# A hybrid attention and linear-attention layer in fp32 pairs on one core: both gate-weight splits in one unit, the last tile's splits and first eviction moved, and the first gates on VectorE

## The chip, the core and the metric

The kernel runs on one core of a Trainium2 chip. Its time is the device time of one execution in microseconds; the kernel before has three timed runs, and one further execution was profiled. In what follows TensorE (PE) multiplies matrices, ScalarE (ACT), VectorE (DVE) and GpSimd (POOL) do the elementwise work, and SyncE (SP) issues the DMAs.

## The reference, cut to what matters

One layer of a decoder takes 2048 prompt tokens (16 tiles of 128) and 8 sequences of 8 sampled tokens (64 rows, the seventeenth tile, called NB in the code).

```python
h = rms_norm(x, g_mix_pre)
proj = jnp.einsum('btd,de->bte', h, w_in)
q, k, v, gq, gk, gv, gr, glr = jnp.split(proj, points, axis=-1)
attn = swa_banded(q, k, v, sinks)                       # group A: window of 128, 8 heads, 2 kv heads
log_a = jax.nn.log_sigmoid(glr @ w_gk2 + b_gk) / 16
o, s_new = gla_chunked(gq, gk, gv, log_a, s0)           # group B: gated linear attention, 4 heads
o = rms_norm(o, g_gla) * jax.nn.silu(gr)                # the output gate
mix = concat([attn, o]) @ w_out
x = x + rms_norm(mix, g_mix_post)
x = x + rms_norm(mlp(rms_norm(x, g_ffn_pre)), g_ffn_post)
```

Everything is wanted in fp32. Each fp32 operand of a large product is kept as a high part, rounded to TensorE's format, and a low part, the remainder; a product is then three matmuls (high with high, high with low, low with high).

## The kernel before, in words

The kernel goes through four stages: attention on all tiles (group A), gated linear attention (GLA, group B) with the output projection at its end, the MLP's two halves, and their ends. TensorE, and in the attention stage ScalarE and VectorE too, go through their instructions in the order in which the program issues them (the class InOrder adds that order by hand). GpSimd, SyncE and, in the GLA stage, the plain ScalarE and VectorE instructions are ordered by a planner, which goes by the order of the program as a priority and by its own estimate of when an operand will be ready.

**Attention (L798 on).** Each tile has four units, two query heads each. A unit (`unit`, L466) is a generator of steps: copy the sinks into the score tile `s` (GpSimd), score products `sc`, row minima (VectorE), exponentials (ScalarE), normalisation (ScalarE and VectorE), transposes `pT`, the high part `ph` (ScalarE), the low part `pl` (VectorE), the value products `av` (which need `ph`, then `pl`), `rest` (ScalarE) and the output `mo`. The loop runs three units interleaved (`behind`, `now`, `ahead`), and between their steps it calls `run(fill, n)`: n matmuls of a list of products that need nothing of the units. In tiles 0 to 13 the list is the projections of later tiles; from tile 14 on it is `projecting` (L611), the products of GLA's columns. The letters T, A, X, S, B, C name places within a unit; the dictionary A_PLAN tells at which unit and letter each side task stands, so `klo0` (L449, the low part of the keys for the next tile: VectorE, then the copy on GpSimd, L451) at unit 3, T.

**Gate weights.** The weights of GLA's columns are in four chunks of 384 columns and eight rows of 128 (chunks 0 and 1 are G_EARLY, 2 and 3 G_LATE). From tile 3 on, each tile loads two raw pieces (`load_gw`, L255, two buffers `wg_raw`), and `split_some` (L767) splits one at unit 1, letter A, and one at unit 1, letter B. A split (L258) is a multiplication by the gain on GpSimd (L262), the copy to the high part on ScalarE, and the subtraction for the low part on GpSimd (L264), the last reader of the raw piece; for two pieces of chunk 0 and for all late ones it is one ScalarE and one VectorE instruction (L222). In the last tile (i = 15) one late piece is split at letter B of every unit, and each split issues the load of a further piece.

**`projecting`** makes one chunk of one tile's columns in 24 products and then evicts the PSUM bank on ScalarE, scaled by the row norms. Tiles 0 and 1 get chunks 0 and 1 within the attention stage and chunks 2 and 3 from its end on. The 64 sampled rows are computed with high and low rows side by side, and the eviction first folds the two (L211: ScalarE, then VectorE).

**Sampled units (L899).** Four further units attend over the caches of the sampled sequences. In the first unit of each half of the sequences the cached keys are transposed on TensorE and copied by ScalarE to `kc`, and the score products `ssc` need that copy.

**GLA (`gla`, L1123).** For each tile: transposes of q and k, seven level sums (`level_sums`, L1056: per level two ScalarE exponentials and two VectorE additions, each waiting for the other engine), the output gate (`gate`, L998: five steps on ScalarE and VectorE and two multiplications of 128x512 on GpSimd, L1007 and L1009), score products per level, their placement into AH and AT (VectorE, L1072 and L1183; the list `put` holds the copy to AT), the new state S (L1189), and the outputs `o`. The normalised and gated output `og` is transposed (`ogT`) in the next tile. `gla` yields numbers of products to be run between its parts (G_FILL = 34, 14, 16, 8, 20 and, for tile 0's first, 66). At the end of the first GLA tile the sampled rows' GLA (`gla_sample`, L1215) joins in as a side task; its gate is the same function. The instructions under `tc.issue_after(put[0].ins)` are ordered behind that instruction on its engine.

Of the kernel before, what the change touches and what calls it, by code (L numbers as in the profile page):

```python
# [15 lines left out]
AF = mybir.ActivationFunctionType  # L16
ALU = mybir.AluOpType
# [4 lines left out]
P = 128  # L22
# [3 lines left out]
NB = T // P  # L26
# [15 lines left out]
NL = len(LEVELS)  # L42
# [22 lines left out]
G_FILL = (34, 14, 16, 8, 20)  # L65
G_FIRST_FILL = 66
# [75 lines left out]
def hybrid_step_kernel(ctx: ExitStack, tc: tile.TileContext, I, O):  # L142
    nc = tc.nc
# [11 lines left out]
    def rows(i):  # L155
        return min(P, NTOK - i * P)
# [7 lines left out]
    te, ac, dv = (InOrder(tc, engine) for engine in (nc.tensor, nc.scalar, nc.vector))  # L164
# [4 lines left out]
    def bank(shape, kind, name):  # L169

        return ps.tile(shape, F32, tag=kind, name=name, bufs=1 if kind in "de" else 2)
# [25 lines left out]
    rstd_all = cpool.tile([P, NTILE], F32, name="rstd_all")  # L197
# [13 lines left out]
    def folded(out, p_, scalar=nc.scalar, vector=nc.vector):  # L211

        scalar.activation(out, p_[NS:], AF.Copy)
        vector.tensor_tensor(out, out, p_[:NS], op=ALU.add)  # L214
        return out
# [394 lines left out]

    def projecting(i, xT, chunks, act=nc.scalar):  # L611

        n = rows(i)
        for c in chunks:
            p_ = bank([P, 512], "a", f"gproj_{i}_{c}")
            _, wh, wl = gw[c]
            products = ((xT[1], wh), (xT[1], wl)) if i == NB else ((xT[0], wh), (xT[0], wl), (xT[1], wh))
            for k in range(KT):
                for u, (x, w) in enumerate(products):
                    te.matmul(  # L620
                        p_[:, :G_N], x[:, k, :], w[:, k, :],
                        start=k + u == 0, stop=k == KT - 1 and u == len(products) - 1,
                    )
                    yield
            if i not in gps:
                gps[i] = gp_pool.tile([P, G_W], F32, tag="gp", name=f"gp_{i}", bufs=2)
            out = gps[i][:n, c * G_N : (c + 1) * G_N]
            src = folded(out, p_[:, :G_N]) if i == NB else p_[:, :G_N]
            act.activation(out, src, AF.Copy, scale=rstd_all[:n, i : i + 1])
            projected.add((i, c))  # L630

    def load_cache(name, c):
# [45 lines left out]
    def run(products, n=None):  # L678
        deque(products if n is None else islice(products, n), 0)
# [87 lines left out]
    def split_some(n):  # L767

        for _ in range(min(n, len(weights))):
            c, k, raw, stage = weights.popleft()  # L770
            split_gw(c, k, raw)
            if stage and late:
                weights.append((*load_gw(*late.popleft(), *stage), stage))
# [3 lines left out]
    fill = chain.from_iterable(project(i, c) for i in range(2, NTILE) for c in range(2))  # L777
# [20 lines left out]
    for i in range(NB):  # L798
        if i + 4 < NTILE:
            load_x(i + 4)  # L800
        if i == NB - 1:
            wa_pool.release()
            w_pools.append(open_gw(G_LATE))
            for n in range(4):
                stage = ("w_raw", 2) if n % 2 else ("x", 2)
                weights.append((*load_gw(*late.popleft(), *stage), stage))
        elif i >= 3:
            for _ in range(min(2, len(early))):
                weights.append((*load_gw(*early.popleft()), None))
        store()  # L810
        if i == 4:
            nc.sync.dma_start(gain_d.rearrange("a d -> (a d)"), I["g_mix_post"][0])
            wgk, msk, smsk, dmsk, onehot, ggla = load_consts()
        if i == NB - 4:
            nc.sync.dma_start(smask, I["c_smask"])
            cached.update({(name, 0): load_cache(name, 0) for name in "kv"})
        if i >= NB - 2:
            t = i - NB + 2
            gxTs[t] = load_T(t, x_place(t))
            fill = chain(fill, projecting(t, gxTs[t], G_EARLY, ac))  # L820
        new = i + 3 < NTILE
        todo["turn"] = lambda: run(rotate(i + 1))
        if i + 2 < NTILE:
            todo["first"] = lambda: take_first(i + 2)
            todo["rest"] = lambda: todo.update(vl=take_rest(i + 2))
        if new:
            todo["junk"] = lambda: todo.update(rstd=x_norm(i + 3))

        def do(u, phase):
            for name, at in A_PLAN:  # L830
                if name == "x0" and i == 0:
                    at = 0, "C"
                if at == (u, phase) and name in todo:
                    todo.pop(name)()

        for u in range(4):
            next(now)
            do(u, "T")
            next(behind, None)
            next(now)  # L840
            do(u, "A")
            if u == 1 and i < NB - 1:
                split_some(1)
            later = next(queue)
            next(later)
            run(fill, A_FILL[u][0])
            next(behind, None)
            if u != 3:
                next(behind, None)
            run(fill, A_FILL[u][1])  # L850
            if u == 0:
                next(now)
            if u < 2 and new:
                hi, todo[f"x{u}"] = x_half(i + 3, u)
                hi()
            elif u == 2:
                todo.update(heads_T(i + 1))
            do(u, "X")
            run(fill, A_FILL[u][2])
            if u:  # L860
                next(now)
            do(u, "S")
            if u == 3:
                next(behind, None)
            next(behind, None)
            next(ahead)
            next(now)
            do(u, "B")
            if u == 1 or i == NB - 1:
                split_some(1)  # L870
            next(now)
            do(u, "C")
            behind, now, ahead = now, ahead, later
    for left in todo.values():
        left()
    store()
    fill = chain(fill, *(projecting(t, gxTs[t], G_LATE, ac) for t in G_FIRST))

    def ranks_T(pair, out):
# [18 lines left out]

    for n in range(4):  # L899
        later = next(queue, None)  # L900
        next(now)
        next(behind)
        if n == 0:
            cached["k", 1] = load_cache("k", 1)
        run(fill, 10)
        if n == 2:
            first_ranks()
        next(now)
        next(behind)
        next(behind)  # L910
        if n == 2:
            cached["v", 1] = load_cache("v", 1)
            z0 = first_decays()
        if later:
            next(later)
        run(fill, 13)
        next(now)
        next(behind, None)
        split_some(4)
        if ahead:  # L920
            next(ahead)
        next(now)
        behind, now, ahead = now, ahead, later
# [74 lines left out]
    def gate(i, gp, n):  # L998

        gr = gp[:n, 1024:1536]  # L1000
        t = next(sgs) if n == P else s_sg
        nc.scalar.activation(t[:n], gr, AF.Abs)
        nc.scalar.activation(t[:n], t[:n], AF.Exp, scale=-1.0)
        nc.scalar.activation(t[:n], t[:n], AF.Ln, bias=1.0)
        nc.vector.scalar_tensor_tensor(t[:n], gr, 0.0, t[:n], op0=ALU.min, op1=ALU.subtract)
        nc.scalar.activation(t[:n], t[:n], AF.Exp)
        nc.gpsimd.tensor_tensor(t[:n], t[:n], gr, op=ALU.mult)  # L1007
        t4 = t[:n].rearrange("p (h d) -> p h d", h=4)
        nc.gpsimd.tensor_tensor(t4, t4, ggla[:n].unsqueeze(1).to_broadcast([n, 4, P]), op=ALU.mult)  # L1009
        return t  # L1010

    def qk_T(i, gp, n, kind="d"):
# [110 lines left out]
    def gla(i, gp, og=iter(())):  # L1123
# [6 lines left out]
        kt = qk_T(i, gp, P)  # L1130
        dec = next(decs)
        following = decayed(i + 1) if i < NB - 1 else iter(())
        yield G_FILL[0] if i else G_FIRST_FILL, True
        deque(og, 0)
        put_diagonal(i, AH, gp, P)
        for l, b in enumerate(LEVELS):
            if l < NL - 1 or i == 0:
                level_sums(before, after, dec, l, b)
            else:
                with tc.issue_after(put[0].ins):  # L1140
                    level_sums(before, after, dec, l, b)
            if l == NL - 1:
                kd = next(kds)
                pair = i // 2 + 1 if i % 2 == 0 and i < NB - 2 else 0
                turned = keys_decayed(after, kt, next(kdTs), P, "e", kd, pair)
                nc.scalar.activation(dec[:, NL], before, AF.Exp, scale=1.0 / 16)
            weighted(XK, XQ, dec, kt, qz, l, b)
        next(turned)
        deque(following, 0)
        yield G_FILL[1], True  # L1150
        assert {(i, c) for c in range(4)} <= projected
        sg = gate(i, gp, P)
        yield G_FILL[2], True
# [284 lines left out]
    fill = chain(ending_, products())  # L1438
# [819 lines left out]
```

## Time and profile before

| what | us |
|---|---|
| median of three runs | 2193.89 |
| lowest and highest | 2193.14, 2196.88 |
| the profiled execution | 2193.01 |
| its span, first to last instruction | 2191.2 |
| TensorE busy in the span | 2156.9 |
| VectorE, ScalarE, GpSimd busy | 1530.7, 1219.1, 257.7 |

In the profile, L12 is line 12 of the kernel; an instruction is named by its output and inputs (`sc<-kh,qh`), and L131 is the line of the helper that issues everything that is ordered by hand. A row of a timeline gives the start, the duration, the engine, the line, the operation, the tiles and shapes, and in brackets the idle time of the engine before it with what ended it. A row of the view of waits gives who waited for what: total, times, longest. PE busy is counted from a matmul's start to the end of its result, and matmuls overlap; a short wait can hide under the one before.

### The profile page before, as it was taken

What the parts mean: (1) busy time and instruction counts of PE and PEld (TensorE: products, weight loads), DVE (VectorE), ACT (ScalarE), POOL (GpSimd) and SP (SyncE); (2) the same over time, 40 slices, a digit from 0 to 9 for tenths busy, and PEclk for the clock granted to TensorE, in tenths of its full rate; (3) what the DMA queues carried; (4) which work ended last, traced back from release to release, by engine and by line L of the source; (5) the groups of instructions that cost most, each with busy time, mean ns of one, the idle gap of its engine ahead of it and who ended that gap; (6) DMA issues with size and microseconds to landing.
All of it is one profiled execution on the core that took longest, in us unless ns stands there. A gap on an engine that the chain in (4) does not pass through costs nothing.

```text
span 2191.2 us, 34210 instructions
## 1 busy us (share of the span) xinstructions
PE 2156.9 (98%) x11784; PEld 1864.8 (85%) x11784; DVE 1530.7 (70%) x3199; ACT 1219.1 (56%) x2626; POOL 257.7 (12%) x414
## 2 busy tenths in 40 slices
PE   8999999999999999999999999999999999999998
PEld 7999989999998888788888887888888888888886
DVE  5988968777785765888888555548676666555566
ACT  5888867566664444555555544435445455444454
POOL 2566512121111100000000000000000000000000
PEclk9999999999999999999999999999999999999999
DMA  7344332224337765877777776758554433766685
GB/s 229 133 144 150 103 104 66 68 71 150 131 126 239 235 205 193 263 240 257 272 258 249 249 237 220 242 181 269 179 182 158 153 136 134 241 202 195 194 271 185
DMA packets 240314, 411.54 MB, mean 188 GB/s; under 512 B 25924, under 2 KB 142124, under 8 KB 236028
## 3 DMA queue, kind: packets, MB, share of 16 engines
q1 hardware_dynamic: 240140, 409.35, 56.6%
q8 instruction: 93, 1.52, 0.3%
q14 instruction: 81, 0.66, 0.1%
HBM read 265.82 MB, written 143.99 MB: 187 GB/s over the span
## 4 chain that ended last, share of the span: by engine, by line
PE 89%; ACT 3%; DVE 3%; DMA 2%; POOL 1%; issue 1%; SPq 0%; DVEq 0%; POOLq 0%; ACTq 0%
PE dn L131 27%; PE gproj L131 11%; PE uc L131 8%; PE uX L131 7%; PE out L1328 7%; PE proj L131 5%; PE ud L131 4%; PE ub L131 4%; PE ue L131 4%; PE sam L131 1%; PE dsam L131 1%; PE o L131 1%; PE sc L131 1%; PE out L131 1%; PE av L131 1%; PE pT L131 1%
## 5 line engine op out<-in xcount | busy, mean ns | idle before, releaser
L131 PE MATMUL dn<-o0t,o0s 128*128 128x512 f32 x896 | 349.3, 390 | 2.1 <-ACT f L2026 1.0
L131 PE MATMUL dn<-o1t,o0s 128*128 128x512 f32 x896 | 349.6, 390 | 0.7 <-DVE o1t L220 0.7
L131 PE MATMUL dn<-o0t,o1s 128*128 128x512 f32 x896 | 349.4, 390 | 0.0
L220 DVE TENSOR_TENSOR o1s<-rs,o0s 128x512 fp32r<-128x512 f32 x224 | 154.6, 691 | 230.9 <-ACT o0s L219 225.1
L219 ACT ACTIVATE o0s<-rs 128x512 fp32r<-128x512 f32 x224 | 141.1, 631 | 305.3 <-PE dn L131 285.4
L131 PE MATMUL gproj<-wg,gxh 128*128 128x384 f32 x1024 | 272.5, 342 | 0.3 <-DVE gp_s L214 0.3
L131 PEld LDWEIGHTS dn<-o0t,o0s 128*128 128x128 f32 x896 | 168.2, 188 | 39.8 <-ACT o0t L219 1.6
L131 ACT ACTIVATE st<-st 128x512 f32<-128x512 f32 x224 | 141.2, 630 | 106.7 <-DVE st L131 101.9
L131 PEld LDWEIGHTS dn<-o1t,o0s 128*128 128x128 f32 x896 | 168.2, 188 | 37.7 <-DVE o1t L220 1.9
L131 PEld LDWEIGHTS dn<-o0t,o1s 128*128 128x128 f32 x896 | 168.2, 188 | 35.3
L131 PE MATMUL uc<-H,s 128*128 128x512 f32 x768 | 187.8, 393 | 2.8 <-ACT st L131 2.8
L131 PEld LDWEIGHTS gproj<-wg,gxh 128*128 128x128 f32 x1024 | 183.8, 188 | 4.1 <-issue 3.1
L131 PE MATMUL gproj<-wg,gxl 128*128 128x384 f32 x576 | 186.0, 340 | 0.4 <-DVE gp_s L214 0.4
L131 PE MATMUL uX<-H,w 128*128 128x512 f32 x768 | 185.5, 390 | 0.0
L131 PEld LDWEIGHTS uc<-H,s 128*128 128x128 f32 x768 | 143.7, 189 | 33.6 <-ACT st L131 3.0
L131 PEld LDWEIGHTS uX<-H,w 128*128 128x128 f32 x768 | 144.4, 188 | 30.5
L220 DVE TENSOR_TENSOR o1t<-rt,o0t 128x512 fp32r<-128x512 f32 x224 | 153.1, 684 | 9.0 <-ACT o0t L219 9.0
L1328 PE MATMUL out<-wo,mt 128*128 128x512 f32 x680 | 158.6, 392 | 0.0
L209 POOL TENSOR_TENSOR frs<-rs_v,half 128x1 f32<-128x1 f32 (+1 forms) x13 | 10.1, 786 | 1208.7 <-DMA rt<-t_d 1119.0
L1328 PEld LDWEIGHTS out<-wo,mt 128*128 128x128 f32 x680 | 126.5, 188 | 26.1
L219 ACT ACTIVATE o0t<-rt 128x512 fp32r<-128x512 f32 x224 | 138.1, 618 | 12.0 <-DMA rt<-t_d 8.5
L131 DVE TENSOR_TENSOR st<-st 128x512 f32<-128x512 f32 x160 | 110.6, 691 | 28.5 <-ACT st L131 24.3
(405 smaller groups left out, 4306.9 us busy)
## 6 DMA issues: line engine op xcount, KB each, us to landing
s_d<-st SPq DMA_DIRECT2D x32, 1792.0 KB, 8.1
rs<-s_d SPq DMA_DIRECT2D x224, 256.0 KB, 2.9
raw<-in_w_up SPq DMA_DIRECT2D x64, 512.0 KB, 4.4
rt<-t_d SPq DMA_DIRECT2D x128, 256.0 KB, 3.9
rt<-in_w_down SPq DMA_DIRECT2D x96, 256.0 KB, 3.0
t<-in_w_down SPq DMA_DIRECT2D x64, 256.0 KB, 3.8
t_d<-t SPq DMA_DIRECT2D x32, 512.0 KB, 4.2
hraw<-h_d SPq DMA_DIRECT2D x20, 512.0 KB, 5.1
```

Source lines behind the costliest of these rows:

```text
L131: ins = call(*a, **k)
L209: nc.gpsimd.tensor_tensor(out, v[:n], e, op=ALU.pow)
L219: nc.scalar.activation(hi, src, AF.Copy)
L220: vector.tensor_tensor(lo, src, f32(hi), op=ALU.subtract)
L1328: te.matmul(banks[c], x, w[:, c * 512 : (c + 1) * 512], start=k + u == 0, stop=k == KT - 1 and u == len(products) - 1,)
```

## The change

Six edits. `projecting` holds back the eviction of tile 0's first chunk of each pair until three products of the following chunk are issued. In tiles 0 to 14 both splits stand at unit 1, letter A. In the last tile the four splits stand at letter B of the units 1, 2 (two) and 3. In the sampled units with an even number three of ten products go ahead of the score products. The two multiplications of `gate` go to VectorE for tile 0 and for the sampled rows. In `gla`, tile 1 runs three more products in its first part and three fewer in its second, and tile 2's level sums 4 and 5 join level 6 behind `put`.

```diff
     def projecting(i, xT, chunks, act=nc.scalar):
-        n = rows(i)
+        n, waiting = rows(i), []
         for c in chunks:
...
                     yield
+                    if waiting and (k, u) == (0, 2):
+                        act.activation(*waiting.pop(), scale=rstd_all[:n, i : i + 1])
...
-            act.activation(out, src, AF.Copy, scale=rstd_all[:n, i : i + 1])
+            if act is ac and (i, c) == (0, chunks[0]):
+                waiting.append((out, src, AF.Copy))
+            else:
+                act.activation(out, src, AF.Copy, scale=rstd_all[:n, i : i + 1])
             projected.add((i, c))
...
             do(u, "A")
             if u == 1 and i < NB - 1:
-                split_some(1)
+                split_some(2)
...
             do(u, "B")
-            if u == 1 or i == NB - 1:
-                split_some(1)
+            if u and i == NB - 1:
+                split_some(1 + (u == 2))
...
     for n in range(4):
         later = next(queue, None)
+        run(fill, 3 * (1 - n % 2))
         next(now)
         next(behind)
         if n == 0:
             cached["k", 1] = load_cache("k", 1)
-        run(fill, 10)
+        run(fill, 10 - 3 * (1 - n % 2))
...
-        nc.gpsimd.tensor_tensor(t[:n], t[:n], gr, op=ALU.mult)
+        engine = nc.vector if i in (0, NB) else nc.gpsimd
+        engine.tensor_tensor(t[:n], t[:n], gr, op=ALU.mult)
         t4 = t[:n].rearrange("p (h d) -> p h d", h=4)
-        nc.gpsimd.tensor_tensor(t4, t4, ggla[:n].unsqueeze(1).to_broadcast([n, 4, P]), op=ALU.mult)
+        engine.tensor_tensor(t4, t4, ggla[:n].unsqueeze(1).to_broadcast([n, 4, P]), op=ALU.mult)
...
-        yield G_FILL[0] if i else G_FIRST_FILL, True
+        yield G_FILL[0] + 3 * (i == 1) if i else G_FIRST_FILL, True
...
-            if l < NL - 1 or i == 0:
+            if l < (4 if i == 2 else NL - 1) or i == 0:
                 level_sums(before, after, dec, l, b)
             else:
                 with tc.issue_after(put[0].ins):
...
-        yield G_FILL[1], True
+        yield G_FILL[1] - 3 * (i == 1), True
```

## The prediction

> **What bounds the kernel now.** I read the page first, then the waits of TensorE alone, from 60 us (behind the start-up) to 400 us (the parts that the diff touches), then the timelines of each engine around each wait.
>
> ```profile
> span 2191.2 us, 34210 instructions
> PE 2156.9 (98%) x11784; PEld 1864.8 (85%) x11784; DVE 1530.7 (70%) x3199; ACT 1219.1 (56%) x2626; POOL 257.7 (12%) x414
> ```
> ```profile
> PE sc L131 <- POOL kl L451: 2.6, 3, 0.9
> PE ssc L131 <- ACT kc L131: 0.9, 2, 0.5
> PE pT L131 <- ACT s L131: 0.8, 2, 0.6
> PE gproj L131 <- DVE gp_s L214: 0.7, 2, 0.4
> PE av L131 <- DVE pl L131: 0.7, 2, 0.5
> PE o L131 <- DVE S L1189: 0.6, 1, 0.6
> PE ogT L131 <- DVE og L1098: 0.3, 1, 0.3
> ```
> TensorE is busy for 98% of the span, and its order is fixed by hand. No product is removed here, so the change can only win back waits like these seven groups (columns: total, times, longest): 6.6 us idle, 14 waits. That caps the gain. The column understates a wait a little, since the matmul before it still counts as busy while its result drains:
>
> ```profile
> 168.31 0.36 PE L131 MATMUL sc<-kh,qh 128*128 128x256 f32 x1
> 169.58 0.39 PE L131 MATMUL sc<-kl,qh 128*128 128x256 f32 x1 [0.91 <-POOL kl L451]
> ```
> The second score product starts 1.27 us behind the first, of which 0.36 is the first one's own row and 0.91 is idle. Part of that 0.36 is drain and not pace (a matmul of 384 columns, quoted below, holds the next one up by only 0.17), so I price a wait at its idle time plus 0.2. Fourteen waits then cost 6.6 + 14 x 0.2 = 9.4 us, the most that this change can give.
>
> **The gate splits of the middle tiles** (two in unit 1, phase A, in place of one each in A and B).
>
> ```profile
> 159.91 1.01 POOL L264 TENSOR_TENSOR wg<-wg_raw,wg 128x384 fp32r<-128x384 f32 x1
> 161.93 0.19 POOL L474 COPY s<-sink 128x2 f32<-128x2 f32 x1 [1.02 <-PE pT L131]
> 162.20 1.01 POOL L264 TENSOR_TENSOR wg<-wg_raw,wg 128x384 fp32r<-128x384 f32 x1
> ```
> ```profile
> 160.94 0.33 SPq L232 DMA_DIRECT2D wg_raw<-in_w_in  x1
> 161.36 0.38 SPq L324 DMA_DIRECT2D xt_d<-xh  x1
> 163.24 0.79 SPq L232 DMA_DIRECT2D wg_raw<-in_w_in  x1
> ```
> ```profile
> 167.05 0.83 POOL L262 TENSOR_TENSOR wg_raw<-wg_raw,gcol 128x384 f32<-128x384 f32 x1 [0.90 <-DMA wg_raw<-in_w_in]
> ...
> 169.24 0.29 POOL L451 CAST kl<-kl 64x128 fp32r<-64x128 f32 x1
> ```
> This is a chain. The second subtraction (162.20 to 163.21) frees the raw buffer; SyncE issues the next load at 163.24; GpSimd, in order, waits for its landing until 167.05 with the multiplication for the *next* tile, and only then makes the copies of the keys, the last at 169.24, for which the score product waits. In the change the second ScalarE copy stands right behind the first:
>
> ```profile
> 159.32 0.51 ACT L131 ACTIVATE wg<-wg_raw 128x384 fp32r<-128x384 f32 x1
> 160.10 0.38 ACT L131 ACTIVATE rest<-av 64x256 f32<-64x256 f32 x1 [0.27 <-PE av L131]
> ```
> It runs from about 159.8 to 160.3, mostly in the 0.27 that ScalarE idles, so `rest` comes at most 0.2 later and the work behind it is relieved of the old copy. The second subtraction then follows the first at 160.95, in the 1.02 us in which GpSimd idles for pT, and ends at 161.95 in place of 163.21: 1.25 earlier. Both loads still pass the same stores on SyncE's queue. Landing 1.25 earlier, the multiplication would start at 165.8, but the one ahead of it on GpSimd ends at about 166.2 (167.05 less the 0.90 of idle), so 0.9 of 1.25 is won here. Three waits of 2.6 in total cost 3.2; I take nine tenths, 2.9, and 0.4 (an estimate: the drain of 0.2 twice) for two neighbouring tiles whose wait for the same copy is too short for the view: **3.3 us**. The bounds are 0 (the landing does not move) and 3.6 (all five go). What is late next? A tile with two splits and hardly this wait shows room:
>
> ```profile
> 202.00:218.00 16.00, 15.93 (x111) 15.45 (x110) 14.39 (x50) 14.48 (x40) 10.68 (x20) 1.00 0.46 156
> ```
> TensorE is busy 15.93 of 16.00 us there, VectorE 14.39 and ScalarE 14.48, so these two are not yet the bound.
>
> **The last tile.** Two edits meet. First, the eviction of tile 0's first gate chunk:
>
> ```profile
> 285.14 0.58 ACT L131 ACTIVATE gp<-gproj,rstd_all 128x384 f32<-128x384 f32 x1
> 285.75 0.38 ACT L131 ACTIVATE rest<-av 64x256 f32<-64x256 f32 x1
> 286.03 0.49 ACT L131 ACTIVATE s<-s,den 128x256 f32<-128x256 f32 x1
> ```
> It stands ahead of the normalised scores, whose transposes are the 0.6 wait of "pT". Moved three products on, it falls into the next unit, where ScalarE idles for av: 0.58 won, the same for the second chunk group nothing (no wait there). Second, the split of unit 0 leaves the path to `pl`:
>
> ```profile
> 289.33 0.45 PE L131 MATMUL av<-pl,vv 128*64 128x256 f32 x2 [0.23 <-DVE pl L131]
> ```
> That wait goes: 0.35 with the drain. But unit 2 now holds two splits ahead of its own `pl`:
>
> ```profile
> 295.04 0.62 DVE L131 SCALAR_TENSOR_TENSOR wg<-wg_raw,gcol,wg 128x384 fp32r<-128x384 f32 x1 [0.53 <-ACT wg L131]
> 295.58 0.48 DVE L131 CUSTOM_DVE_ANT_0 s<-sc,amask,sink 128x256 f32<-128x256 f32 x1
> ```
> VectorE goes from one to the next in 0.54 (295.04 to 295.58), so the second pushes the minima and `pl` behind them back by 0.54. TensorE takes this `pl` as it comes, so 0.54 is lost. Together 0.58 + 0.35 - 0.54 = **0.4 us**, bounds -0.2 and 0.9.
>
> **Products ahead of the sampled scores.** Both `ssc` waits (0.9 idle, 1.3 with drain) are for a copy that ScalarE makes meanwhile. Three products of
>
> ```profile
> 282.75 0.51 PE L131 MATMUL gproj<-wg,gxh 128*128 128x384 f32 x2
> 283.10 0.34 PE L131 MATMUL gproj<-wg,gxl 128*128 128x384 f32 x1
> ```
> (two in 0.51, one alone 0.34: 0.17 each) fill 0.52 of each: **1.0 us**. Seven products remain behind the scores in place of ten; the VectorE work that they covered has slack of about their length. Bounds 0.5 and 1.3.
>
> **First gates on VectorE, and the first GLA tiles.** Tile 0's two gate multiplications sit on GpSimd while VectorE walks the level sums:
>
> ```profile
> 336.43 1.43 POOL L1009 TENSOR_TENSOR sg<-sg,ggla 128x512 f32<-128x512 f32 x1
> ```
> ```profile
> 336.42 0.28 DVE L1039 TENSOR_TENSOR XK<-dec,kt 128x128 f32<-128x128 f32 x1
> 336.63 1.38 DVE L1066 TENSOR_TENSOR before<-before 128x128 f32<-128x128 f32 x1
> ```
> ```profile
> 338.04 0.32 ACT L1062 ACTIVATE dec<-before 128x128 f32<-128x128 f32 x1 [1.19 <-DVE before L1066]
> 338.38 0.49 ACT L213 ACTIVATE gp_s<-gproj 64x384 f32<-64x384 f32 x1
> ```
> A 128x128 operation that takes 0.28 took 1.38 and ended 0.15 behind GpSimd's. ScalarE waited 1.19 for it, and the eviction that frees TensorE's bank stood behind (the "gproj <- DVE gp_s" waits, 0.7 idle in two). On VectorE a multiplication of this size costs
>
> ```profile
> 345.74 0.68 DVE L1178 TENSOR_TENSOR qd<-qz,dec 128x512 f32<-128x512 f32 x1
> ```
> so two cost 1.36, part of it between level sums where VectorE idles for ScalarE, and they give back twice 1.1 if both blocked it. I count one of the two waits, **0.5 us**; bounds -0.5 (the operations land ahead of the level sums and nothing is given back) and 1.1. [...]
>
> The "ogT" wait of 0.3 has three more products put in front of it (0.52): 0.5 won with its drain. The "o <- S" wait of 0.6:
>
> ```profile
> 372.90 0.29 DVE L1065 TENSOR_TENSOR after<-after,before 128x128 f32<-128x128 f32 x1
> ...
> 374.30 1.58 DVE L1072 COPY_PREDICATED AH<-c,gl 128x128 f32<-128x128 uint8 x4
> ```
> Tile 2's level sums 4 and 5 (from 372.90, four operations in step with ScalarE) stand ahead of tile 1's score placement (374.30); ordered behind it, the placement starts 1.2 us or more earlier, and with it the state update for which TensorE waits: 0.7 of 0.8 won. The sums are paid later, where TensorE wants nothing of tile 2 for most of a tile. **1.2 us**, bounds 0.5 and 1.3.
>
> **Sum**: 3.3 + 0.4 + 1.0 + 0.5 + 1.2 = 6.4 us. The profiled execution took 2193.0 us, 1.8 around its span; less 6.4 it is 2186.6. It lies 0.9 below the median of the runs, 2193.9, so I forecast **2187.5 us**, a gain of 0.29%. The gain should reach the end, for behind 400 us TensorE stays the bound.
>
> **Rivals.**
> 1. *The load's landing does not move* (a store on the same engines holds it up, or the planner places the subtraction behind the `s` copy, which waits for pT until 161.93 anyway). For it: 163.24 to 167.05 is 3.8 us, long for a load. Against it: GpSimd's idle hole is exactly there. The 3.3 go: 2187.5 + 3.3 = 2190.8 us, within 0.2%. Chance 0.18.
> 2. *The gain is given back* at the hand-over to the MLP, or by small new waits as VectorE and ScalarE near 15 of 16 us per tile: 2192 to 2194 us. For it: those two are over 90% busy; against it: the tile quoted above. Chance 0.10.
> 3. *Slower*: SyncE's order changes, and the second load falls behind the 512 KB store of `xl` as well as that of `xh`. At the 156 GB/s of the tile above a store lasts 3.4 us. TensorE already waits for this chain, so each microsecond past 167.05 is paid in full in about four tiles: 4 x 3.4 = 13.6, less the 3.1 us of the other parts, 2204 us. It decides from 1.9 us of delay on ((3.1 + 4.4) / 4). Against it: the load is ready earlier than before, not later. Chance 0.06.
>
> **Chances and range.** Forecast (2185.5 to 2189.4) 0.62; still faster, by the second `gp_s` wait and short waits below the view's threshold, 0.04; rival 1 0.18, rival 2 0.10, rival 3 0.06. About 0.2% (4.4 us) is what a measurement of this kernel can tell from no change, so faster means below 2189.5: 0.66; same 0.28; slower 0.06. The range runs from the cap of 9.4 us, 2184.5, to 2192.0, which takes in rival 1 and part of rival 2.
>
> **What would show it.** Right: second subtraction directly behind the first, the second raw load issued about 1 us after the first in place of 2.3, "sc <- POOL kl" gone or below 0.5; `gp` behind the exponentials in the last tile; both `ssc` waits below 0.2; tile 0's `before` at 0.3 us; "o <- S" and "ogT" gone; a new av wait of about 0.4 idle in the last tile's unit 2. Wrong: the multiplication on wg_raw still starting 3.8 us or more behind the first load's, VectorE's level sums of tile 0 longer than before, or new TensorE waits in tiles 3 to 10.

## The result, and the profile after

| | before | after |
|---|---|---|
| median of the timed runs | 2193.61 us (8 runs) | 2186.99 us (8 runs) |
| lowest and highest | 2191.23, 2201.41 | 2186.18, 2192.31 |
| the profiled execution, and its span | 2193.01, 2191.2 | 2189.12, 2187.3 |

The ratio of the times is 0.997, with a 95% interval of 0.9958 to 0.9982: the change gains 6.6 us by the medians, against the 6.4 of the sum and the 2187.5 us of the forecast. In a second set of runs (`change_again` below) it gained 6.1 us. So the total is right. Its terms are not all right: some were worth more than the sum says, some less, and part of what was won is gone again by the end. That these errors cancel to 0.2 us is luck.

The page of the kernel after, its span and TensorE's line:

```profile
span 2187.3 us, 34212 instructions
PE 2156.4 (99%) x11784; PEld 1866.2 (85%) x11784; DVE 1530.3 (70%) x3203; ACT 1221.7 (56%) x2626; POOL 251.7 (12%) x410
```

As many matmuls as before, as busy as before, in a span shorter by 3.9 us. TensorE's waits from 60 to 400 us, the same view as in the prediction (total, times, longest):

```profile
PE pT L131 <- DVE s L131: 0.4, 1, 0.4
PE av L131 <- DVE pl L131: 0.4, 1, 0.4
PE pT L131 <- ACT s L131: 0.2, 1, 0.2
```

Of 6.6 us of idle time 1.0 is left. The av wait is the new one that was foretold for the last tile's unit 2. The first line is new, in tile 4, where the prediction named a new wait as a sign against it. It stands in place of an av wait of 0.5 that is gone, and costs nothing net.

The chain of the gate splits in the same tile as in the prediction, on GpSimd and then on SyncE's queue:

```profile
160.00 1.99 POOL L264 TENSOR_TENSOR wg<-wg_raw,wg 128x384 fp32r<-128x384 f32 x2
162.02 0.19 POOL L474 COPY s<-sink 128x2 f32<-128x2 f32 x1
165.16 1.61 POOL L262 TENSOR_TENSOR wg_raw<-wg_raw,gcol 128x384 f32<-128x384 f32 x2 [2.96 <-DMA wg_raw<-in_w_in]
...
168.14 0.29 POOL L451 CAST kl<-kl 64x128 fp32r<-64x128 f32 x1
```
```profile
161.05 1.30 SPq L232 DMA_DIRECT2D wg_raw<-in_w_in  x2
162.44 0.39 SPq L324 DMA_DIRECT2D xt_d<-xh  x1
```

Both subtractions now stand ahead of the `s` copy, as predicted. Both loads go out back to back, now *ahead* of the store of `xh`, where before the second was issued behind it (163.24). The prediction had said that both loads would still pass the same stores. The score products follow each other without a wait:

```profile
168.36 0.36 PE L131 MATMUL sc<-kh,qh 128*128 128x256 f32 x1
168.55 0.32 PE L131 MATMUL sc<-kl,qh 128*128 128x256 f32 x1
```

To find where the time came from, I compare positions: when TensorE reaches the same matmul in each trace. For example, the first transposes of the queries of tiles 3 and 11, before and then after (the starts of the first and the last stand at the end of each line's times):

```profile
L131 PE MATMUL pq<-ident,rot x4: 272/273/273, 82.2 to 82.6; 128*128 128x128 f32 x4
L131 PE MATMUL pq<-ident,rot x4: 272/273/273, 214.0 to 214.4; 128*128 128x128 f32 x4
```
```profile
L131 PE MATMUL pq<-ident,rot x4: 271/272/273, 83.6 to 83.9; 128*128 128x128 f32 x4
L131 PE MATMUL pq<-ident,rot x4: 272/272/273, 211.8 to 212.1; 128*128 128x128 f32 x4
```

That is 131.8 us before and 128.2 after: 3.6 won between the two tiles. The table in the next part does the same, from unrounded starts, for four stretches that separate the edits: A, from tile 3 to tile 11 (the paired splits); B, from the 25th to the 133rd product of the GLA columns (last tile, sampled scores); C, from the 193rd to the 340th (gates, ogT); D, from the 340th to the 500th (level sums). The last column is everything from the first output projection (`out<-wo`) to the last matmul, the hand-over to the MLP among it. What lies between the stretches is left out; the 0.3 us that nine of the thirteen runs lose between the 500th product and the first output projection are the largest part of it behind A.

### The profile page after: what moved, and what is told of

Same layout as the page of the kernel before. It is cut to its first block, busy times and chain, and to the rows that moved or that the text cites. A ratio compares the mean times of both kernels' runs of the same rounds, so it can differ in the third digit from the quotient of the medians.

```text
span 2187.3 us, 34212 instructions
## 1 busy us (share of the span) xinstructions
PE 2156.4 (99%) x11784; PEld 1866.2 (85%) x11784; DVE 1530.3 (70%) x3203; ACT 1221.7 (56%) x2626; POOL 251.7 (12%) x410
## 4 chain that ended last, share of the span: by engine, by line
PE 92%; DVE 3%; ACT 2%; DMA 1%; issue 1%; POOL 0%; SPq 0%; DVEq 0%; ACTq 0%; POOLq 0%
PE dn L131 27%; PE gproj L131 12%; PE uc L131 8%; PE uX L131 8%; PE out L1335 7%; PE proj L131 6%; PE ud L131 4%; PE ub L131 4%; PE ue L131 4%; PE sam L131 1%; PE dsam L131 1%; PE sc L131 1%; PE pT L131 1%; PE o L131 1%; PE av L131 1%; PE out L131 1%
```

## The experiments

Us won against the kernel before, by stretch. A star marks a stretch in which the granted clock of that run was down for 3.4 us more than in the run of before (two stars: 6.8 us), a plus one where it was down for 3.4 us less; each costs or brings 1.5 to 1.7 us, an estimate from stretch D (-0.3 in `change_again` beside 1.2 in the change, -1.0 beside 0.6 in the two executions of `gates_on_pool`) and from half its length. The drops themselves are shown at the end.

| run | A | B | C | D | MLP |
|---|---|---|---|---|---|
| the sum of the prediction | 3.3 | 1.4 | 1.0 | 0.7 | 0 |
| the change, profiled | 3.6 | 1.4 | 2.1 | 1.2 | -2.8* |
| `change_again` | 3.6 | 1.4 | 2.1 | -0.3* | -0.7 |
| `pair_only` | 2.9 | 0.0 | -0.1 | -3.1** | 0.1+ |
| `all_but_pair` | 0.9 | 1.4 | 2.1 | 1.2 | -1.2 |
| `gates_on_pool` | 3.6 | 1.4 | 0.4 | 0.6 | 0.7 |
| `gates_on_pool_timed` | 2.6 | 1.4 | 0.4 | -1.0* | -3.5* |
| `last_tile_as_before` | 3.2 | 1.4 | 2.1 | -0.4* | -3.5* |
| `eviction_in_place` | 2.3 | 0.8 | 2.1 | -0.3* | -1.3 |
| `no_products_ahead` | 2.3 | 0.5 | 2.1 | -0.3* | -1.5 |
| `level_sums_free` | 1.1 | 1.4 | 2.1 | -1.5* | 1.9+ |
| `no_shift` | 3.3 | 1.4 | 2.1 | 1.2 | -1.1 |
| `more_raw` | 1.6 | 0.0 | 0.2 | -3.5** | 1.7+ |
| `change_more_raw` | 0.1 | 1.4 | 2.1 | 1.2 | -0.7 |

Stretch B repeats to 0.1 us wherever its code is the same, and C does with the gates on VectorE; with the code of before C runs from -0.1 to 0.2. A does not repeat, and this was the first surprise.

### The paired splits: `pair_only`, `all_but_pair`

`pair_only` is the kernel before with this one edit; `all_but_pair` is the change without it.

```diff
             if u == 1 and i < NB - 1:
-                split_some(1)
+                split_some(2)
...
-            if u == 1 or i == NB - 1:
+            if i == NB - 1:
                 split_some(1)
```

> The kernel before, with one edit alone: in tiles 0 to 14 both splits stand at unit 1, letter A. Theory (the second raw load is issued sooner, lands sooner, and GpSimd reaches the copies of the keys sooner): the wait of sc for POOL kl falls from 2.6 us in three to nothing, TensorE is 3.3 to 3.6 us ahead of the kernel before when tile 11 begins, counted from the beginning of tile 3, and the time falls by about as much, to a ratio of 0.9984. Rival (the landing does not move): no wait goes, 0 us, ratio 1.000.

Measured: 2192.22 us (11 runs) beside 2194.91 (17 runs), ratio 0.999 (0.9981 to 0.9999): 2.7 us by the medians, 2.9 in stretch A. Its waits on GpSimd's copies of the keys fell from three to one:

```profile
PE sc L131 <- POOL kl L451: 0.6, 1, 0.6
```

> The changed kernel with the pairing in tiles 0 to 14 taken back (one split at A, one at B of unit 1). Theory (the parts add up): TensorE loses nothing and wins nothing between tiles 3 and 11, the three waits of sc for POOL kl are back, and what is left of the gain is that of the other edits, 4 to 5 us by the trace of the changed kernel, ratio 0.998. Rival (the gains overlap, since VectorE and ScalarE near their bound): less than 3 us left, ratio above 0.9986.

Measured: 2188.77 us (7 runs), ratio 0.997 (0.9959 to 0.998): 6.1 us by the medians without the edit that was to bring half of the gain. Stretch A still shows 0.9, and the waits are 1.8 in four, against 2.6 in three:

```profile
PE sc L131 <- POOL kl L451: 1.8, 4, 0.8
```

The split sequence of A is that of before in this kernel, and TensorE was expected to win nothing there. So part of what A shows in the change need not be the pairing's. The medians do not add up either: 2.7 for the pairing alone and 6.1 for the rest would make 8.8, and the change has 6.1 to 6.6. What the pairing adds to the other edits is thus not resolved by the times; A alone shows it, and A needs more than one draw.

### What varies in A: `gates_on_pool` twice, `change_again`

`gates_on_pool` leaves attention untouched and undoes the edit of the gates, so its stretch A is that of the change.

```diff
-        engine = nc.vector if i in (0, NB) else nc.gpsimd
+        engine = nc.gpsimd
```

> The changed kernel with all gate multiplications on GpSimd again. Theory (each engine locks the other out): the level sums of tile 0 that stand beside the two multiplications take 1.2 to 1.4 us again in place of 0.3, the eviction behind them is late, and TensorE loses 0.5 to 1.1 us in waits on gproj between its 193rd and 257th gate product. Rival (the slow level sums of the kernel before were an accident): no row above 0.5 us, and no wait.

> The change with the gates' multiplications all on GpSimd, once more, timed. By the positions of TensorE in the first look at it the gates on VectorE are worth 1.3 to 1.7 us by the 300th product: median 2188.3 to 2188.7 us beside 2187.0 of the change. Rival: the later stages take it back (the hand-over to the MLP swallows what comes early), and both medians are the same within 0.5 us.

One kernel, two executions, 3.6 and 2.6 us in A. The first and then the second execution, GpSimd at tile 8:

```profile
178.34 0.83 POOL L262 TENSOR_TENSOR wg_raw<-wg_raw,gcol 128x384 f32<-128x384 f32 x1 [1.32 <-DMA wg_raw<-in_w_in]
180.50 0.83 POOL L262 TENSOR_TENSOR wg_raw<-wg_raw,gcol 128x384 f32<-128x384 f32 x1 [1.33 <-DMA wg_raw<-in_w_in]
```
```profile
178.11 0.83 POOL L262 TENSOR_TENSOR wg_raw<-wg_raw,gcol 128x384 f32<-128x384 f32 x1 [1.34 <-DMA wg_raw<-in_w_in]
181.67 0.83 POOL L262 TENSOR_TENSOR wg_raw<-wg_raw,gcol 128x384 f32<-128x384 f32 x1 [2.74 <-DMA wg_raw<-in_w_in]
```

The loads were issued at 175.84 and at 175.60. Counted from there, the first piece is taken after 2.5 us in both, the second after 4.7 and after 6.1, and in the second execution TensorE waits:

```profile
184.20 0.39 PE L131 MATMUL sc<-kl,qh 128*128 128x256 f32 x1 [0.91 <-POOL kl L451]
```

So the landing of the second load is what differs, from one execution to the next of the same instructions.

What holds it up can be read from the DMA packets of the traces. In both executions one packet of 16 KB on a queue that the profile calls `instruction` starts at 177.87 us, while the load is under way. The view of DMA from 177.8 to 179.9 us (packets, MB, share of 16 engines' time), in the first and then in the second execution:

```profile
q8 instruction: 1, 0.02, 3.7%
```
```profile
q8 instruction: 1, 0.02, 6.3%
```

That is 1.2 and 2.1 us of one engine. The load has 128 packets; spread evenly, that is eight for each of 16 engines. In the second execution the last eight start at 179.98 us, when the instruction packet ends (180.00), and end at 181.01; GpSimd takes the piece at 181.67. In the first all of the load's packets have ended at 179.99. In the traces with paired splits GpSimd idles for 2.4 us or more ahead of the second multiplication seven times (three in `level_sums_free`, one each in `gates_on_pool_timed`, `eviction_in_place`, `no_products_ahead` and `change_more_raw`). In all seven the last eight packets start within 0.02 us of the end of an instruction packet of 2.0 to 2.4 us. That they stand behind it on one engine is inferred from these times, since the packets do not name their engine; why the instruction packet takes longer in some executions stays open.

> The changed kernel unaltered, beside the next kernel on the same chip, and as one more draw of the landing of the second raw load. Theory (the load's landing varies from execution to execution, the rest of the change is steady): the gain between tile 3 and tile 11 lies anywhere from 1.1 to 3.6 us, while the products ahead (1.0 us between tile 16 and the 133rd gate product) and the gates (1.3 us or more by the 300th) come out as in the other run of it. Rival (the landing is steady and the other variants' edits moved it): 3.6 us again. Time near 2187.0 us, 6 to 7 below the kernel before.

Measured: 2188.27 us (5 runs) beside 2194.32 (12 runs), ratio 0.9968 (0.9955 to 0.998). Its A is 3.6 again, so the change itself was not seen to vary in two draws; that the landing varies rests on the other kernels, `gates_on_pool` above all. Over the ten traces that have the paired splits with two buffers A runs from 1.1 to 3.6, with a mean of 2.85; the two that have neither the pairing nor added buffers show 0 (before, against itself) and 0.9. I put the edit at about 2.4 us (an estimate: 2.85 less half of 0.9) and not at 3.3.

The gates' timed run gives 2188.51 us (8 runs), ratio 0.9971 (0.996 to 0.9981), and is told further down.

### An earlier load: `more_raw`, `change_more_raw`

If the second load is late because the subtraction frees its buffer late, more buffers must help. In every other tile the raw pieces go to the buffers of the caches, which are free then: in the kernel before (`more_raw`) and in the change (`change_more_raw`).

```diff
-            for _ in range(min(2, len(early))):
-                weights.append((*load_gw(*early.popleft()), None))
+            for n in range(min(2, len(early))):
+                stage = (f"cache_{'kv'[n]}", 1) if i % 2 else ("w_raw", 2)
+                weights.append((*load_gw(*early.popleft(), *stage), None))
```

> The kernel before with its splits where they were, but with the raw pieces of odd tiles in two other buffers, so that a load no longer waits for the subtraction of the tile before. If the late landing of the second load is what holds GpSimd up, the waits of sc for POOL kl go without any move of a split: 3 us or more between tiles 3 and 11. If it is the amount or the order of GpSimd's work, they stay: 0 to 0.5 us.

> The change, and besides the raw pieces of every other tile in the buffers of the caches, which are free at that time, so that a load no longer waits for the subtraction of the tile before. Theory (what is left of the wait of the keys' copies is the second load, which is issued only when the second subtraction frees the buffer): the waits of sc for kl go whatever the landing, the gain between tile 3 and tile 11 is 3.3 to 4.0 us, and the median is 0 to 1 us below that of the change. Rival (what is left is the queue's order, the loads' share of the DMA engines or GpSimd's own work): sc waits for kl as in the change, 1.1 to 3.6 us, and the same median within 0.5 us.

Measured: `more_raw` 2191.6 us in one run, A 1.6. That is between theory and rival, and it is a sum of two things. The three waits of the kernel before for the copies of the keys are gone without any move of a split, 3.1 us in all, as the theory has it; a new wait for such a copy in tile 5, with what it delays, takes 1.6 back. In the tile of the prediction's chain, SyncE and then GpSimd:

```profile
162.27 0.33 SPq L232 DMA_DIRECT2D wg_raw<-in_w_in  x1
```
```profile
166.25 0.29 POOL L451 CAST kl<-kl 64x128 fp32r<-64x128 f32 x1
167.02 0.83 POOL L262 TENSOR_TENSOR wg_raw<-wg_raw,gcol 128x384 f32<-128x384 f32 x1 [0.48 <-DMA wg_raw<-in_w_in]
```

The load still goes out behind the second subtraction, and GpSimd takes the piece 4.8 us later (3.8 before). But here the planner has put the copies of the keys *ahead* of that multiplication, and TensorE does not wait. So the wait of before takes two things: a late landing, and a place of the multiplication ahead of the copies in GpSimd's order.

`change_more_raw` took 2187.74 us (5 runs) beside the change's 2188.27 on the same chip, ratio to before 0.9969 (0.9956 to 0.9981). Its A is only 0.1, and its waits on the keys' copies:

```profile
PE sc L131 <- POOL kl L451: 1.6, 3, 0.9
```

The theory's numbers are missed, but the edit did not do what it was to do either. (That the time is no worse is no merit of the edit: the profiled execution won 3.3 us ahead of tile 3, where the clock did not drop and tile 1 was short; both are told at the end.) GpSimd and then SyncE at tile 8:

```profile
173.59 1.97 POOL L264 TENSOR_TENSOR wg<-wg_raw,wg 128x384 fp32r<-128x384 f32 x2
175.61 0.19 POOL L474 COPY s<-sink 128x2 f32<-128x2 f32 x1
177.07 0.83 POOL L262 TENSOR_TENSOR wg_raw<-wg_raw,gcol 128x384 f32<-128x384 f32 x1 [1.28 <-DMA wg_raw<-in_w_in]
180.87 0.83 POOL L262 TENSOR_TENSOR wg_raw<-wg_raw,gcol 128x384 f32<-128x384 f32 x1 [2.97 <-ACT s L131]
```
```profile
174.62 1.29 SPq L232 DMA_DIRECT2D wg_raw<-in_w_in  x2
```

The load still goes out when the first subtraction ends (173.59 + 1.03), exactly as in the change (160.00 and 161.05 above). The planner used the added buffers to start the loads one tile earlier, at the beginning, and here the multiplications went forward with them: GpSimd takes each one right behind a load just issued, ahead of the copies of the keys. So what a load freed from the subtraction would bring was not measured, in either kernel. The second piece was late in this trace too. (The multiplication reads the raw piece and the gains alone, so the 2.97 that the view puts down to `s` is the load's.)

### The last tile: `eviction_in_place`, `last_tile_as_before`

```diff
-            if act is ac and (i, c) == (0, chunks[0]):
+            if False:
```

> The changed kernel with every gate-chunk eviction where it was. Theory: the wait of pT for ACT s in the last tile's unit 0 grows from 0.2 to 0.8 us with its drain, and 0.6 us are lost between the 25th and the 49th gate product, nothing elsewhere. Rival (the wait in unit 0 went with the split): nothing is lost.

One run, 2188.09 us. B loses 0.6 (1.4 to 0.8), and the prediction's line of the wait of pT for ACT s is back (0.8 in two, the longest 0.6). 0.58 was predicted for it. In the change ScalarE evicts behind the exponentials:

```profile
285.92 0.56 ACT L131 ACTIVATE gp<-gproj,rstd_all 128x384 f32<-128x384 f32 x1
286.55 0.38 ACT L131 ACTIVATE rest<-av 64x256 f32<-64x256 f32 x1
```

Next the splits of the last tile, one at letter B of each unit as before, the eviction still moved:

```diff
-            if u and i == NB - 1:
-                split_some(1 + (u == 2))
+            if i == NB - 1:
+                split_some(1)
```

> The changed kernel with one late split in every unit of the last tile, as before; the eviction stays moved. Theory (two splits ahead of one pl cost 0.54 us, and the split of unit 0 costs 0.35 at most): the wait of av in unit 2 (0.4 idle) goes, one of 0.2 to 0.35 comes back in unit 0, and TensorE is 0.2 to 0.3 us further ahead at the first sampled unit. Rival (the move paid): 0.3 us or more behind.

One run, 2190.75 us, most of its distance in two drops of the clock. B is 1.35 beside 1.43: the move is worth 0.1, not the -0.2 of the sum (0.35 - 0.54). The av wait of unit 0, 0.23 idle before, grows to what unit 2's is in the change. This row is of `last_tile_as_before`, the next of the change:

```profile
285.84 0.45 PE L131 MATMUL av<-pl,vv 128*64 128x256 f32 x2 [0.38 <-DVE pl L131]
```
```profile
294.27 0.45 PE L131 MATMUL av<-pl,vv 128*64 128x256 f32 x2 [0.39 <-DVE pl L131]
```

The two edits interact: once the eviction is gone from unit 0, TensorE gets there 0.6 earlier and its wait for `pl` is longer. (That this is the reason is argued from the two rows; no run has the move of the split alone.)

### Sampled scores: `no_products_ahead`

```diff
-        run(fill, 3 * (1 - n % 2))
...
-        run(fill, 10 - 3 * (1 - n % 2))
+        run(fill, 10)
```

> The changed kernel with ten products behind the sampled scores again. Theory: both waits of ssc for ACT kc are back, 0.5 us each, 1.0 us lost between the 49th and the 133rd gate product. Rival (the copy to kc comes earlier anyway with the splits moved): 0.3 us or less.

One run, 2188.99 us. B loses 0.9, and the line of both waits is that of before again (0.9 in two, the longest 0.5). The predicted 1.0 holds.

### The gates: `gates_on_pool` and its timed run

Stretch C loses 1.7 us in both executions (2.1 to 0.4), of which 0.5 was predicted. In `gates_on_pool` GpSimd's two multiplications and VectorE's additions of the level sums lie so:

```profile
330.42 1.29 POOL L1014 TENSOR_TENSOR sg<-sg,gp 128x512 f32<-128x512 f32 x1 [3.43 <-ACT sg L1012]
331.79 1.43 POOL L1016 TENSOR_TENSOR sg<-sg,ggla 128x512 f32<-128x512 f32 x1
```
```profile
330.63 1.23 DVE L1072 TENSOR_TENSOR after<-after,before 128x128 f32<-128x128 f32 x1
331.98 1.38 DVE L1073 TENSOR_TENSOR before<-before 128x128 f32<-128x128 f32 x1
```

Each multiplication has one addition stretched over it, ending 0.15 behind it. In the change, the same two lines and the first multiplication, all on VectorE:

```profile
330.92 0.28 DVE L1072 TENSOR_TENSOR after<-after,before 128x128 f32<-128x128 f32 x1
331.23 0.29 DVE L1073 TENSOR_TENSOR before<-before 128x128 f32<-128x128 f32 x1
331.44 0.68 DVE L1014 TENSOR_TENSOR sg<-sg,gp 128x512 f32<-128x512 f32 x1
```

0.28 and 0.29 in place of 1.23 and 1.38. That the additions last that long beside the multiplications is measured; what holds them up is not shown. The prediction took only one of the two `gp_s` waits; both went. Before, they held TensorE up by 0.54 and 0.48 beyond the normal distance, with 0.1 each for the next matmul, 1.2 in all, and a shorter wait of `o` for `AT` (0.3 in two matmuls) was below the view's threshold.

With the gates back on GpSimd the two waits are there again:

```profile
PE gproj L131 <- DVE gp_s L214: 0.9, 2, 0.6
```

And a wait of 0.4 idle of `ds` for ScalarE's `kd` appears in stretch D, which with its neighbour costs 0.7 of its 1.2. By positions the gates are worth 2.4 us at the 500th product (1.7 in C, 0.7 in D, from unrounded starts). By the medians they are worth 0.2 (2188.51 and 2188.27, whose runs spread over 7.5 and 4.8 us). In the last column the two executions of `gates_on_pool` differ by more than that (0.7 won, and 3.5 lost of which the clock has 1.5 to 1.7). So how much of the 2.4 is left at the end is not shown.

### GLA: `level_sums_free`, `no_shift`

```diff
-            if l < (4 if i == 2 else NL - 1) or i == 0:
+            if l < NL - 1 or i == 0:
```

> The changed kernel with tile 2's level sums 4 and 5 free to go ahead of tile 1's score placement. Theory: the wait of o for DVE S is back, 0.6 us idle and 0.8 with the drain, lost between the 340th and the 500th gate product. Rival (the gates on VectorE had already moved the level sums early enough): 0.2 us or less.

One run, 2188.67 us. The wait for the state is back, larger than before's 0.6 since TensorE arrives earlier:

```profile
PE o L131 <- DVE S L1196: 0.9, 1, 0.9
```

It holds TensorE up by 1.02; D without its clock drop is 0.0 to 0.2 beside 1.2. So the order of the level sums is worth 1.0, of which 0.7 was predicted.

```diff
-        yield G_FILL[0] + 3 * (i == 1) if i else G_FIRST_FILL, True
+        yield G_FILL[0] if i else G_FIRST_FILL, True
...
-        yield G_FILL[1] - 3 * (i == 1), True
+        yield G_FILL[1], True
```

> The change without the three products that tile 1 runs earlier. Prediction's term: the wait of ogT for og comes back, 0.3 idle, about 0.5 us with its drain. Rival: the gates on VectorE have moved og forward too, and no wait comes back: the same pace as the change between the 340th and the 500th product within 0.1 us, clock dips left out.

One run, 2186.55 us. C and D are those of the change to 0.02, and no ogT wait comes back: the rival is right. The gates on VectorE bring `og` early enough by themselves. In `gates_on_pool` the wait is gone too, there by the three products. Either edit removes it, so its 0.5 was won once, and beside the gates the three products add nothing.

## Why the prediction came out

One count first: the prediction says 14 waits, and the groups of its view add up to 13, so its cap is 9.2 us and not 9.4. No term hangs on it.

**The paired splits** (3.3 predicted, about 2.4 measured). The mechanism is as predicted: the second subtraction moved into the hole, its load went out 1.2 earlier, the three waits went. What failed is the step "landing 1.25 earlier": I let the second load land as long after its issue as it had in one execution, and in the late landings its last eight packets start only when an instruction packet ends. The step that the prediction did not see is GpSimd's order: with the copies ahead of the multiplication (`more_raw`) the landing costs nothing. Rival 1 (the landing does not move) holds in some tiles of some executions, and there the wait stays. Rival 3, the store ahead of the load, went the other way: the loads are now issued ahead of it.

**The last tile** (0.4 predicted; 0.6 and 0.1 measured for its two edits). Eviction right; the price of the split that moved was set against a wait of 0.35 (0.43 by the prediction's own rule of idle time plus 0.2) that the eviction's own gain lengthens to 0.54.

**Products ahead** (1.0; 0.9 measured). Right.

**The gates** (0.5 predicted, 1.7 measured in C by the 340th product and 0.7 in D). The term that was mis-sized most. The prediction counted one of two waits without a reason in the trace to halve it, and it could not see what lay under the threshold of the view of waits.

**GLA** (1.2 predicted: 0.5 for ogT and 0.7 for the level sums; taking the edits back costs 0 and 1.0). The level sums were mis-sized because the wait that they remove grows when everything ahead of it gets faster. The ogT wait did go, but the gates alone remove it too.

**Behind 400 us** (nothing given back was predicted; part is lost). Rival 2 put the loss at the hand-over to the MLP. The waits there do change: TensorE's wait of `xnT` for `ht` is 1.0 us before, 1.6 in the change, 1.0 in `change_again`, 1.3 in `all_but_pair` and 0.6 in `pair_only`. But from the first output projection to 987 us `change_again` wins 0.1 and the change loses 0.6, the clock drop left out, and over all runs it goes from 0.6 lost to 0.7 won. What the runs lose, they lose behind it, at two places, about 1520 and 1870 us. TensorE's waits at the first, from 1420 to 1540 us, before and in `pair_only`:

```profile
PE dn L131 <- DVE f L1954: 0.4, 1, 0.4
```
```profile
PE dn L131 <- DVE f L1954: 1.8, 1, 1.8
```

And at the second, from 1850 to 1890 us in `pair_only`, where the kernel before has no such line:

```profile
PE dn L131 <- ACT o0t L219: 0.6, 1, 0.6
```

The first wait is 0.6 in the change, 0.2 in `change_again`, and 0.3 and 1.8 in the two executions of `gates_on_pool`; the second is 0.5 to 0.7 in both traces of the change, in `all_but_pair` and in the second execution of `gates_on_pool`, and absent in the first. So it is not the gates on VectorE that bring them, and they differ between executions of one kernel. Whether the kernel before has them in other executions is not known, since one of its executions was traced. So "the gain should reach the end" did not hold in the six traces with the gates on VectorE and no mark in the last column, which lose 0.7 to 1.5 us there; that the change causes the loss is not shown, for `pair_only` loses as much once its plus is taken out.

By the 500th product both traces of the change are 8.3 us ahead, the clock left out (3.6, 1.4, 2.1 and 1.2), against the 6.4 of the sum; with 2.4 for A, the estimate above, it is 7.1. The medians show 6.6 and 6.1. So the terms of the first 400 us were too small on the whole, the pairing's by the estimate too large, and what is missing at the end, part of it in the two waits above, made up for that.

## What to carry to other kernels

Where two engines' rows of the same length end together, as a 0.28 us addition that takes 1.38 beside a GpSimd multiplication, count every wait behind them and not a cautious half. A term that hangs on a DMA's landing is a draw: give it the spread of the landings in the trace, since the same kernel had 3.6 and 2.6 us here. And ask what stands behind the late piece in its engine's order: the copies of the keys needed nothing of the load, and ahead of the multiplication they cost nothing. Price waits in order of time: each one that goes makes TensorE come earlier to the next, which then is longer (0.23 to 0.38, 0.6 to 0.9).

## What the runs showed of the hardware

In the stretches below the granted clock drops to half for 3.4 us or twice that, at places that change from run to run, and this is one of the things that limit a comparison at 0.2%. In slices of 1 us from 36 to 45 us it was 1.00, 0.87, 0.50, 0.50, 0.50, 0.92, 1.00, 1.00, 1.00 before, and 0.82, six times 0.50, 0.77, 1.00 in the change: what lacks to 1.00 adds up to 1.71 and 3.41 us, or 3.4 and 6.8 us at 0.50. Two stretches of the kernel before, two of the change, and one each of `change_more_raw` and `change_again` (length, then busy time and instructions of PE, PEld, DVE, ACT and POOL, the granted clock, the DMA's share and GB/s):

```profile
30.00:50.00 20.00, 17.41 (x104) 16.43 (x103) 10.43 (x45) 11.95 (x37) 9.18 (x15) 0.91 0.47 157
905.00:930.00 25.00, 21.25 (x93) 17.01 (x92) 19.45 (x28) 13.64 (x23) 0.00 (x0) 0.93 0.77 256
```
```profile
30.00:50.00 20.00, 17.41 (x93) 16.37 (x93) 9.95 (x41) 10.63 (x33) 9.18 (x15) 0.83 0.44 150
905.00:930.00 25.00, 20.95 (x86) 16.68 (x85) 18.80 (x28) 15.27 (x27) 0.00 (x0) 0.86 0.68 227
```
```profile
30.00:50.00 20.00, 17.41 (x113) 16.55 (x112) 11.79 (x49) 13.88 (x44) 10.49 (x20) 1.00 0.58 195
```
```profile
385.00:405.00 20.00, 20.00 (x175) 18.34 (x174) 12.66 (x43) 8.99 (x30) 1.32 (x2) 0.91 0.16 54
```

A mean of 0.91 over 20 us is 3.6 us at half the clock, 0.83 is 6.8, and 1.00 is none: the same stretch holds none of it, 3.4 us or twice that. By these means the change's profiled execution had 20 x 0.08 + 25 x 0.07 = 3.4 us less of the full clock than that of before; TensorE lost 1.4 us by it ahead of tile 3 and 1.5 at the hand-over to the MLP. That is most of what separates the 3.9 us which its profile shows from the 6.6 of the medians. What brings a drop on is not shown. Before, the one at 37.7 us comes behind three microseconds (34 to 37) in which TensorE is busy for 0.47; in `change_again` the one at 389 us (0.57 over the four microseconds from there, 1.00 over the 24 ahead) comes with TensorE busy for all of the 20 us around it, though with many matmuls of 16 and 64 columns.

A row that is long beside one of the other engine, as at the gates, shows once more, and here it varies which engine has it. In tile 1 a subtraction of VectorE (`c_raw<-c_raw,wgk`) and a multiplication of GpSimd start within 0.01 us of one another in the twelve traces without added buffers. The VectorE row in the kernel before and in `eviction_in_place`, whose code is the same there:

```profile
52.78 1.15 DVE L653 TENSOR_TENSOR c_raw<-c_raw,wgk 32x256 f32<-32x256 f32 x1
```
```profile
52.83 0.42 DVE L658 TENSOR_TENSOR c_raw<-c_raw,wgk 32x256 f32<-32x256 f32 x1
```

In ten of the twelve VectorE's takes 1.15 us and GpSimd's 0.87; in `eviction_in_place` and `no_products_ahead` 0.42 and 1.16 (1.15). With VectorE's next such operation (1.82 or 1.02) this makes the tile 1.5 us shorter for TensorE, a draw that has nothing to do with the change. In the two traces with added buffers the subtraction stands elsewhere, and the tile is 1.7 and 1.8 us shorter.
